# Transposing both heads of a query block before either copy out of PSUM, in a one-core streaming encoder layer

## The chip, the cores and the metric

One core of one Trainium2 chip runs the whole program. The metric is device time in microseconds, median of several runs; the kernel before was run three times.

## The reference

One trunk layer of a streaming encoder for 1024 prompt frames and 64 sample frames, 1024 features, all in fp32:

```python
h = rms_norm(x, norm_mix)
glu_a, glu_b, q, k, v, gates = jnp.split(h @ w_in, SPLITS, axis=-1)
u = glu_a * jax.nn.sigmoid(glu_b)
c, conv_state = causal_dwconv(u, conv_hist, conv_dw, conv_dw_b)          # width 31
c = jax.nn.silu(layer_norm(c, conv_ln_g, conv_ln_b)) @ w_conv_out
a, k_state, v_state = attend(q, k, v, rel_table)                          # 16 heads of 64
a = a @ w_att_out
x = x + (g[..., :D_MODEL] * c + g[..., D_MODEL:] * a) @ w_out
x = x + (jax.nn.gelu(dwconv(up)) * gate) @ w_ffn_down
x = x + jax.nn.sigmoid(rms_norm(x) @ w_ple_gate) * (p @ w_ple_proj)
```

`attend` lets each frame see its own chunk of 64 frames and the eight chunks before it: scores plus a bias by clipped distance, a softmax, and the weighted sum of values. A final norm follows.

## The kernel before

The data lie feature-major: a tile holds 128 features by all 1088 frames. Every big product is done in three passes on TensorE, with weights and activations each split into a high and a low part (`mm3`, lines 154 to 166: high times high, high times low, low times high, over 8 blocks of 128 features). Frames are taken in groups of 384, 384 and 320 columns. ScalarE makes the high parts of the weights (line 134), VectorE the low parts (135).

The first stage, up to about 1 ms, computes the input projection, job by job: a GLU gate and value pair (`gb`, `ga`), gates (`s`), and q, k and v for one pair of heads. It runs two other things beside the projection. One is the depthwise convolution: 31 taps of about 1.4 us on VectorE for each feature block (line 329), later its layer norm on VectorE and ScalarE, kept in a list `bg` that is worked off a little at a time. The other is attention for the pair of heads that is ready: 8 blocks of 128 queries and one of 64 sample queries, held in `pipe`. For each of 8 pairs the 9 query blocks run during the `gb`, `ga` and `s` jobs.

The order is written out by hand: `tick` (line 544) is called twice in each column group of a job, once after the first four feature blocks (12 matmuls) and once after the group's eviction. Ticks alternate. At an even one a new query block's scores are issued (`step_S`), then the weighted sum of an older block (`step_PV`), then the exponentials of the new one (`step_E`). At an odd one an older block is transposed (`step_T`), then the newer one's exponentials are scaled by the reciprocal of their sums (`step_R`). So in steady state TensorE does: transposes of block p, half a projection group, scores of block p+2, weighted sum of block p, the rest of the group, and again.

PSUM has eight banks. Two are for the projection, one for the weighted sum, one for small things. The remaining four are one buffer, `ps_st`, tag "st", with one slot. Scores (`s_ps`, line 478) and transposes (`t_ps`, line 506) use it in turn: head 0 has the first two of its banks, head 1 the other two. A new tile in that slot can be written only once all that used the old one is done. The tile layer that records the instructions adds all waits by itself; it looks at a PSUM tile as a whole here. Each engine runs its own instructions in the order of the program.

The steps by name and line: L485 scores (TensorE, `s_ps`), L491 the bias add and row minimum out of PSUM (VectorE, `s`), L501 exponentials (ScalarE), L526 scaling (ScalarE), L511 transposes (TensorE, `t_ps`; a full block has five of 128 x 128 for each head), L514 the copy of a head's transposes to SBUF (ScalarE, `pt`; L516 and L519 for the sample block), L536 the weighted sum (TensorE, `o_ps`), L170 and L171 its split into high and low parts (`aT`). L677, L662 and L666 are evictions of the `s`, `gb` and `ga` jobs. L159, L160, L161 are the three passes of the projection (`pj`).

Of the kernel before, what the change touches and what calls it, by code (L numbers as in the profile page):

```python
# [75 lines left out]
def encoder_step(ctx: ExitStack, tc: tile.TileContext, I, O):  # L76
# [143 lines left out]
    with tc.manual_schedule():  # L220
# [283 lines left out]
        def step_T(st):  # L504
            m, n = st["m"], st["n"]
            ps = ps_st[0].tile([P, 2, 1024], F32, tag="st", name="t_ps")
            st["pt"] = []
            for h, s in enumerate(st["s"]):
                for b in range(st["nb"]):
                    w = min(P, n - b * P)  # L510
                    nc.tensor.transpose(ps[0:w, h, b * P:b * P + m], s[0:m, b * P:b * P + w], ident[0:m, 0:m])  # L511
                pt = at.tile([P, 640], F32, tag="pt", name="pt", bufs=2)
                if m == P:
                    nc.scalar.activation(out=pt[:, 0:n], in_=ps[:, h, 0:n], func=AF.Copy)  # L514
                else:
                    nc.scalar.activation(out=pt[:, 0:512].rearrange("p (b q) -> p b q", q=P)[:, :, 0:m],  # L516
                                         in_=ps[:, h, 0:512].rearrange("p (b q) -> p b q", q=P)[:, :, 0:m],
                                         func=AF.Copy)
                    nc.scalar.activation(out=pt[0:64, 512:512 + m], in_=ps[0:64, h, 512:512 + m], func=AF.Copy)  # L519
                st["pt"].append(pt)  # L520
# [23 lines left out]
        def tick(base=1.95):  # L544
# [24 lines left out]
            if flip is not None:  # L569
                step_T(flip)  # L570
                stages["pv"].append(flip)
# [1078 lines left out]
```

## Time and profile before

| what | value |
|---|---|
| runs of the kernel before | 2201.48, 2203.5, 2205.72 us; median 2203.5 |
| the profiled execution | 2199.4 us, its span 2197.3 us |
| granted TensorE clock over the span | 0.99 |
| TensorE, matmuls | 2094.6 us busy, 95% |
| TensorE, weight loads | 2012.2 us busy, 92% |
| VectorE | 1320.1 us busy, 60% |
| ScalarE | 829.8 us busy, 38% |
| GpSimd | 224.2 us busy, 10% |
| attention's transposes | first at 98.8 us, last at 996.8 us |

PE is a matmul on TensorE, PEld a weight load on it; the two overlap. DVE is VectorE, ACT ScalarE, POOL GpSimd, SP SyncE. A group of instructions is given by line, engine, operation, and output and input tiles; "idle before" is the time its engine stood still just ahead of it, and the arrow names what ended that wait. Matmul ends are modelled, so short gaps on PE are less certain than starts.

### The profile page before, as it was taken

What the parts mean: (1) busy time and instruction counts of PE and PEld (TensorE: products, weight loads), DVE (VectorE), ACT (ScalarE), POOL (GpSimd) and SP (SyncE); (2) the same over time, 40 slices, a digit from 0 to 9 for tenths busy, and PEclk for the clock granted to TensorE, in tenths of its full rate; (3) what the DMA queues carried; (4) which work ended last, traced back from release to release, by engine and by line L of the source; (5) the groups of instructions that cost most, each with busy time, mean ns of one, the idle gap of its engine ahead of it and who ended that gap; (6) DMA issues with size and microseconds to landing.
All of it is one profiled execution on the core that took longest, in us unless ns stands there. A gap on an engine that the chain in (4) does not pass through costs nothing.

```text
span 2197.3 us, 35659 instructions
## 1 busy us (share of the span) xinstructions
PE 2094.6 (95%) x14696; PEld 2012.2 (92%) x14696; DVE 1320.1 (60%) x2246; ACT 829.8 (38%) x1583; POOL 224.2 (10%) x453
## 2 busy tenths in 40 slices
PE   8989899999999998979999999999999999999997
PEld 6979798988888887869999999999999999999997
DVE  6676676676766645343235457777777763345644
ACT  5352635344545446473012334333333331113421
POOL 4000101101010111111000000000000020000400
PEclk9999999999999999999999999999999999999999
DMA  3312121212121221113533341212212144331011
GB/s 135 106 35 90 64 86 49 94 50 87 51 90 47 92 76 67 58 54 134 200 128 133 118 138 40 89 69 80 89 60 89 71 161 165 123 121 45 11 58 53
DMA packets 64706, 192.54 MB, mean 88 GB/s; under 512 B 8368, under 2 KB 22976, under 8 KB 63200
## 3 DMA queue, kind: packets, MB, share of 16 engines
q1 hardware_dynamic: 43072, 104.00, 13.8%
q0 software_dynamic: 21328, 85.71, 10.9%
q8 instruction: 115, 1.88, 0.4%
q10 hardware_dynamic: 144, 0.56, 0.1%
q14 instruction: 47, 0.39, 0.1%
HBM read 146.18 MB, written 54.01 MB: 91 GB/s over the span
## 4 chain that ended last, share of the span: by engine, by line
PE 82%; ACT 7%; DVE 5%; issue 4%; DMA 1%; POOL 0%; SPq 0%; POOLq 0%; ACTq 0%; DVEq 0%
PE pj L159 15%; PE pj L161 14%; PE pj L160 14%; PE pj L1159 7%; PE pj L1160 7%; PE pj L1158 7%; PE pj L1461 3%; PE pj L1460 3%; PE pj L1459 3%; PE o_ps L536 2%; PE t_ps L511 2%; PE s_ps L485 2%; ACT pt L514 2%; ACT s L501 1%; DVE c L329 1%
## 5 line engine op out<-in xcount | busy, mean ns | idle before, releaser
L159 PE MATMUL pj<-hT,whl 128*128 128x384 f32 (+1 forms) x1296 | 444.3, 343 | 0.7 <-ACT sg L677 0.7
L160 PE MATMUL pj<-hT,whl 128*128 128x384 f32 (+1 forms) x1296 | 427.0, 329 | 0.0
L161 PE MATMUL pj<-hT,whl 128*128 128x384 f32 (+1 forms) x1296 | 426.7, 329 | 0.3 <-DVE whl L135 0.3
L329 DVE SCALAR_TENSOR_TENSOR c<-u,cc,c 128x1118 f32<-128x1118 f32 x240 | 330.7, 1378 | 2.4
L159 PEld LDWEIGHTS pj<-hT,whl 128*128 128x128 f32 x1296 | 246.2, 190 | 14.2 <-issue 10.9
L161 PEld LDWEIGHTS pj<-hT,whl 128*128 128x128 f32 x1296 | 245.8, 190 | 0.6 <-DVE whl L135 0.6
L160 PEld LDWEIGHTS pj<-hT,whl 128*128 128x128 f32 x1296 | 245.9, 190 | 0.0
L1158 PE MATMUL pj<-mp,wq 128*128 128x272 f32 x704 | 204.2, 290 | 5.0 <-ACT ug L1234 2.7
L1160 PE MATMUL pj<-mp,wq 128*128 128x272 f32 x704 | 204.6, 291 | 0.0
L1159 PE MATMUL pj<-mp,wq 128*128 128x272 f32 x704 | 204.4, 290 | 0.0
L135 DVE TENSOR_TENSOR whl<-raw,whl 128x1024 fp32r<-128x1024 f32 (+3 forms) x100 | 115.8, 1159 | 137.0 <-ACT whl L134 136.9
L134 ACT ACTIVATE whl<-raw 128x1024 fp32r<-128x1024 f32 (+3 forms) x100 | 100.1, 1001 | 221.5 <-PE pj L1461 133.7
L491 DVE CUSTOM_DVE_ANT_0 s<-s_ps,bias 128x640 f32<-128x640 f32 (+3 forms) x144 | 90.4, 664 | 145.2 <-PE s_ps L485 145.0
L1135 ACT ACTIVATE wq<-raw 128x512 fp32r<-128x512 f32 x144 | 84.3, 625 | 191.0 <-DVE raw L1144 135.6
L511 PE MATMUL t_ps<-ident,s 128*128 128x128 f32 (+2 forms) x560 | 86.7, 277 | 71.9 <-ACT pt L514 66.8
L511 PEld LDWEIGHTS t_ps<-ident,s 128*128 128x128 f32 (+2 forms) x560 | 61.9, 141 | 92.0 <-ACT pt L514 82.5
L1460 PE MATMUL pj<-gp,whl 128*128 128x384 f32 (+1 forms) x432 | 141.3, 327 | 0.3 <-DVE gp L1369 0.3
L1461 PE MATMUL pj<-gp,whl 128*128 128x384 f32 (+1 forms) x432 | 141.3, 327 | 0.2 <-DVE whl L135 0.2
L1459 PE MATMUL pj<-gp,whl 128*128 128x384 f32 (+1 forms) x432 | 141.0, 326 | 0.0
L1158 PEld LDWEIGHTS pj<-mp,wq 128*128 128x128 f32 x704 | 134.1, 191 | 5.4 <-ACT ug L1234 2.9
L1159 PE MATMUL pj<-bq,wq 128*128 128x272 f32 x480 | 138.6, 289 | 0.0
L1160 PE MATMUL pj<-bq,wq 128*128 128x272 f32 x480 | 138.3, 288 | 0.0
(255 smaller groups left out, 4716.9 us busy)
## 6 DMA issues: line engine op xcount, KB each, us to landing
raw<-in_w_in SPq DMA_DIRECT2D x56, 512.0 KB, 3.5
raw<-in_w_ffn_up SPq DMA_DIRECT2D x44, 512.0 KB, 4.5
q_d<-ug POOLq DMA_DIRECT2D x22, 544.0 KB, 3.0
gp<-q_d POOLq DMA_DIRECT2D x22, 544.0 KB, 7.3
tg<-s_d POOLq DMA_DIRECT2D x16, 544.0 KB, 3.9
aP<-a_d POOLq DMA_DIRECT2D x8, 1088.0 KB, 6.0
a_d<-aT POOLq DMA_DIRECT2D x64, 128.0 KB, 2.2
f_d<-e_d POOLq DMA_DIRECT2D x16, 383.5 KB, 4.9
```

The source lines that it names most:

```text
L135: nc.vector.tensor_tensor(out=hl[:, 1, 0:k, :], in0=raw[:, 0:k, :], in1=hl[:, 0, 0:k, :].bitcast(F32), op=ALU.subtract)
L159: nc.tensor.matmul(ps, lhsT=wsel(hl, 0, k), rhs=r[:, 0, c0:c0 + n], start=(k == 0), stop=False)
L160: nc.tensor.matmul(ps, lhsT=wsel(hl, 0, k), rhs=r[:, 1, c0:c0 + n], start=False, stop=False)
L161: nc.tensor.matmul(ps, lhsT=wsel(hl, 1, k), rhs=r[:, 0, c0:c0 + n], start=False, stop=(k == K - 1))
L329: nc.vector.scalar_tensor_tensor(out=c_t[f], in0=u_t[f][:, j:j + CCOL], scalar=pc("conv_dw", f * CW + j), in1=c_t[f], op0=ALU.mult, op1=AL ...
L511: nc.tensor.transpose(ps[0:w, h, b * P:b * P + m], s[0:m, b * P:b * P + w], ident[0:m, 0:m])
L1158: nc.tensor.matmul(ps, lhsT=q[:, 0, kt, :], rhs=h, start=start and kt == 0, stop=False)
L1159: nc.tensor.matmul(ps, lhsT=q[:, 0, kt, :], rhs=l, start=False, stop=False)
L1160: nc.tensor.matmul(ps, lhsT=q[:, 1, kt, :], rhs=h, start=False, stop=stop and kt == 3)
L1459: nc.tensor.matmul(ps, lhsT=hl[:, 0, k, :], rhs=h, start=k == 0, stop=False)
L1460: nc.tensor.matmul(ps, lhsT=hl[:, 0, k, :], rhs=l, start=False, stop=False)
L1461: nc.tensor.matmul(ps, lhsT=hl[:, 1, k, :], rhs=h, start=False, stop=k == K - 1)
```

## The change

In `step_T` the loop over the two heads is cut in two. The transposes of both heads are issued first, in the same order as before, and then the two copies, in the same order as before.

```diff
             for h, s in enumerate(st["s"]):
                 for b in range(st["nb"]):
                     w = min(P, n - b * P)
                     nc.tensor.transpose(ps[0:w, h, b * P:b * P + m], s[0:m, b * P:b * P + w], ident[0:m, 0:m])
+            for h in range(2):
                 pt = at.tile([P, 640], F32, tag="pt", name="pt", bufs=2)
                 if m == P:
                     nc.scalar.activation(out=pt[:, 0:n], in_=ps[:, h, 0:n], func=AF.Copy)
```

Without the waits, every engine's list of instructions is the same in both programs. What differs is what some of them wait for. On TensorE, around the transposes of one full query block and the next scores, the program before has (in brackets the semaphores of the engines that are waited for):

```order
L511 MATMUL t_ps<-ident,s 128x128 [waits DVE_49,PE_49,Activation_49]
L511 MATMUL t_ps<-ident,s 128x128 x4
L511 MATMUL t_ps<-ident,s 128x128 [waits Activation_49]
L511 MATMUL t_ps<-ident,s 128x128 x4
L159 MATMUL pj<-hT,whl 128x384
...
L161 MATMUL pj<-hT,whl 128x384
L485 MATMUL s_ps<-K,Q 128x320 [waits Activation_49]
L485 MATMUL s_ps<-K,Q 128x320 x11
```

and the changed one, at the same place:

```order
L511 MATMUL t_ps<-ident,s 128x128 [waits DVE_49,PE_49,Activation_49]
L511 MATMUL t_ps<-ident,s 128x128 x4
L511 MATMUL t_ps<-ident,s 128x128 [waits Activation_49]
L511 MATMUL t_ps<-ident,s 128x128 x4
L159 MATMUL pj<-hT,whl 128x384
...
L161 MATMUL pj<-hT,whl 128x384
L485 MATMUL s_ps<-K,Q 128x320 [waits PE_49,Activation_49]
L485 MATMUL s_ps<-K,Q 128x320 x11
```

Nothing moved. The second head's first transpose names ScalarE's semaphore in both, but the count differs: before, it is the count that head 0's copy L514 reaches; now, the one that the scaling L526 of head 1's scores reaches. The scores L485 also name TensorE's own semaphore now, at the count of the last transpose.

On ScalarE, around the copies of one full query block, before (each of the two copies waits for TensorE):

```order
L501 ACTIVATE s,sm<-s,sm 128x640 [waits DVE_49] x2
L677 ACTIVATE sg<-pj,cc 128x320 [waits DMASW4_49,PE_49]
L514 ACTIVATE pt<-t_ps 128x640 [waits PE_49,Activation_49] x2
L526 ACTIVATE s<-s,sm 128x640 [waits DVE_49] x2
L170 ACTIVATE aT<-o_ps 128x128 [waits DMASW7_49,PE_49]
```

and now, with line numbers one higher from the added line on:

```order
L501 ACTIVATE s,sm<-s,sm 128x640 [waits DVE_49] x2
L678 ACTIVATE sg<-pj,cc 128x320 [waits DMASW4_49,PE_49]
L515 ACTIVATE pt<-t_ps 128x640 [waits PE_49,Activation_49]
L515 ACTIVATE pt<-t_ps 128x640 [waits Activation_49]
L527 ACTIVATE s<-s,sm 128x640 [waits DVE_49] x2
L170 ACTIVATE aT<-o_ps 128x128 [waits DMASW7_49,PE_49]
```

The first copy's wait for TensorE is now at the count of the last transpose of head 1, and the second copy waits for TensorE no more.

## The prediction

> **What bounds the kernel now.** I read the page's busy line first, then busy time by stage, then TensorE's waits, then one quiet query block and one disturbed one in the timeline. The page:
>
> ```profile
> PE 2094.6 (95%) x14696; PEld 2012.2 (92%) x14696; DVE 1320.1 (60%) x2246; ACT 829.8 (38%) x1583; POOL 224.2 (10%) x453
> ...
> L511 PE MATMUL t_ps<-ident,s 128*128 128x128 f32 (+2 forms) x560 | 86.7, 277 | 71.9 <-ACT pt L514 66.8
> ```
>
> TensorE is the bound, with 2094.6 of 2197.3 us busy, and about 102.7 us idle. One line, the transposes, has 71.9 of that. By stage (start and end; length; busy time and count of PE, PEld, DVE, ACT, POOL; granted clock; DMA share; GB/s):
>
> ```profile
> 99.00:917.00 818.00, 760.76 (x5502) 699.75 (x5501) 522.47 (x828) 384.33 (x835) 87.67 (x172) 1.00 0.21 69
> 917.00:997.00 80.00, 64.18 (x461) 56.61 (x459) 35.48 (x72) 57.12 (x101) 9.87 (x16) 0.91 0.15 52
> 997.00:2197.00 1200.00, 1179.52 (x8229) 1175.34 (x8228) 696.44 (x1240) 347.22 (x561) 95.70 (x219) 0.99 0.28 99
> ...
> 223.00:287.00 64.00, 56.93 (x452) 49.55 (x450) 43.02 (x78) 39.27 (x85) 8.52 (x15) 1.00 0.17 57
> 287.00:343.00 56.00, 55.92 (x359) 54.49 (x359) 38.23 (x48) 15.57 (x38) 4.48 (x11) 1.00 0.26 90
> ```
>
> The change can act only before 997 us. There, stretches with attention in them (223 to 287) leave TensorE idle for 7 of 64 us; the projections between them (287 to 343) leave 0.1 us. After 997 it is 98% busy. Who it waits for, in the quiet attention stretches (to 917) and in the last one (917 to 997), where ScalarE also carries the layer norm's passes:
>
> ```profile
> PE t_ps L511 <- ACT pt L514: 51.6, 56, 4.4
> PE t_ps L511 <- ACT pt L519: 4.4, 7, 0.6
> PE v_ps L708 <- ACT lnb L384: 1.2, 2, 0.6
> ...
> PE t_ps L511 <- ACT pt L514: 15.2, 8, 2.6
> PE t_ps L511 <- ACT pt L519: 0.6, 1, 0.6
> ```
>
> Total, times, longest. That is 63 waits and 56.0 us to 917, 9 waits and 15.8 us after it: 72, one for each of the 8 x 9 query blocks. Each stands between head 0's transposes and head 1's. A quiet block of full size (start, duration, engine, line, idle before and its releaser):
>
> ```profile
> 501.27 0.64 PEld L511 LDWEIGHTS t_ps<-ident,s 128*128 128x128 f32 x5
> 501.44 0.71 PE L511 MATMUL t_ps<-ident,s 128*128 128x128 f32 x5
> 501.64 0.58 ACT L677 ACTIVATE sg<-pj,cc 128x384 f32<-128x384 f32 x1 [0.38 <-PE pj L161]
> 502.25 0.70 ACT L514 ACTIVATE pt<-t_ps 128x640 f32<-128x640 f32 x1
> 503.00 0.53 PEld L511 LDWEIGHTS t_ps<-ident,s 128*128 128x128 f32 x5 [1.09 <-ACT pt L514]
> 503.00 0.77 PE L511 MATMUL t_ps<-ident,s 128*128 128x128 f32 x5 [0.85 <-ACT pt L514]
> 503.50 0.19 PEld L159 LDWEIGHTS pj<-hT,whl 128*128 128x128 f32 x1
> 503.87 0.70 ACT L514 ACTIVATE pt<-t_ps 128x640 f32<-128x640 f32 x1 [0.92 <-PE t_ps L511]
> 504.47 1.54 ACT L526 ACTIVATE s<-s,sm 128x640 f32<-128x640 f32 x2
> 505.80 0.89 PEld L485 LDWEIGHTS s_ps<-K,Q 64*128 64x128 f32 x12 [0.25 <-issue]
> 508.13 0.82 DVE L491 CUSTOM_DVE_ANT_0 s<-s_ps,bias 128x640 f32<-128x640 f32 x1
> 508.99 0.83 ACT L501 ACTIVATE s<-s,sm 128x640 f32<-128x640 f32 x1 [0.47 <-DVE sm L491]
> 510.34 0.71 PE L511 MATMUL t_ps<-ident,s 128*128 128x128 f32 x5
> ```
>
> Five transposes, a pause of TensorE of 0.85 us while ScalarE copies head 0, five more; then ScalarE in turn idles 0.92 us before copying head 1. The two engines take turns on one four-bank tile, though each head has two banks of its own in it. A block comes every 510.34 - 501.44 = 8.90 us. (Line numbers are those of the kernel before.)
>
> **The pause.** Issue order is the same on all five engines; only waits change. Head 1's first transpose now waits for the scaling L526 of its own scores, made one period earlier, so nothing in front of it is late. Removed per block: by the PE row 0.85 us, by the weight-load row 1.09. The pipe also drains and refills, so I take 0.05 above the PE row. To 917: 56.0 + 63 x 0.05 = 59.2 us. Ends: 56, and 71 if every load gap counted in full, from
>
> ```profile
> PEld t_ps L511 <- ACT pt L514: 65.4, 56, 4.6
> ...
> PEld t_ps L511 <- ACT pt L519: 5.6, 7, 0.8
> ```
>
> **The copies move together.** Head 0's copy now waits for all the transposes. Five loads of 0.14 us take 0.64, so one each 0.125 us; five more delay it by 0.63: it starts at 502.25 + 0.63 = 502.88, the second ends 1.40 later at 504.28, and TensorE sees it some 0.05 us after (502.95 to 503.00 above). Who waits? The next scores, L485, which reuse the same four banks. Their place comes forward too: ten loads from 501.27 end at 502.52, and from the first projection load to theirs it was 503.50 to 505.80, so they want to start at 504.82. Slack about 0.5 us, where it was 505.80 - 504.57 = 1.2. In the groups of 320 columns the half group of twelve matmuls is about a sixth shorter, 0.35 us by proportion, and the slack 0.15. The cover is those twelve projection matmuls; without them each block would pay 1.4 us. Queued behind the copies on ScalarE are the scaling L526, a weight split L134 and the copy aT L170; they come earlier by up to 0.3 us, since ScalarE loses its 0.92 us between copies. GpSimd's and SyncE's queues are not passed by anything.
>
> What does not fit under that cover? The blocks where ScalarE is late already. The longest, at 136.7:
>
> ```profile
> 136.33 4.21 DVE L329 SCALAR_TENSOR_TENSOR c<-u,cc,c 128x1118 f32<-128x1118 f32 x3
> 136.49 0.64 PEld L511 LDWEIGHTS t_ps<-ident,s 128*128 128x128 f32 x5
> 140.63 0.49 ACT L662 ACTIVATE u<-pj 128x384 f32<-128x384 f32 x1 [4.15 <-DVE c L329]
> 141.02 0.70 ACT L514 ACTIVATE pt<-t_ps 128x640 f32<-128x640 f32 x1
> 141.77 1.33 PE L511 MATMUL t_ps<-ident,s 128*128 128x128 f32 x5 [4.40 <-ACT pt L514]
> 145.82 0.89 PEld L485 LDWEIGHTS s_ps<-K,Q 64*128 64x128 f32 x12 [0.25 <-issue]
> ```
>
> Three taps on VectorE hold ScalarE's eviction L662, and the copies stand behind it. After the change they would still run from 141.02 to 142.42, while the scores want 136.49 + 1.25 + 2.30 = 140.04: 2.4 us of the 4.40 come back as a wait of L485. For the other late blocks and the 320-column groups I allow 3 us (some 21 blocks of 63 at 0.1, and a few tenths for the rest; 0 to 10). To 917: 59.2 - 2.4 - 3 = 54 us.
>
> **The new wait.** L485 now also waits on TensorE's own semaphore, an instruction of its own ahead of it in 48 places; the transposes carry such a one already:
>
> ```profile
> L511 PEldq EVENT_SEMAPHORE  x71: 51/51/51, 98.8 to 992.6; - x71
> ```
>
> 51 ns, and at 501.27 no gap in the loads before it. What it waits for is twelve matmuls old. I take nothing; 48 x 0.051 = 2.4 us is the other end.
>
> **The last stretch, 917 to 997.** Here the pauses average 15.8 / 9 = 1.76 us, and the granted clock is 0.91. The rows of one pause:
>
> ```profile
> 926.06 0.64 PE L511 MATMUL t_ps<-ident,s 128*128 128x128 f32 x2 [1.88 <-ACT pt L514]
> 926.81 0.52 PE L160 MATMUL pj<-hT,whl 128*128 128x384 f32 x1
> 927.13 0.52 PE L161 MATMUL pj<-hT,whl 128*128 128x384 f32 x1
> ...
> 929.82 0.33 PE L161 MATMUL pj<-hT,whl 128*128 128x384 f32 x1
> ```
>
> After 1.88 us of idle time matmuls take 0.52 us instead of 0.33 for a while, so a pause costs more than itself; over the stretch up to 0.09 x 80 = 7.2 us. The Trainium skill, "TensorE: Matmul & The Clock Gate", section "HAM oscillation — how this bites in real kernels", has the clock fall only when a gap crosses a window of about 3.4 us. By that rule only the 4.40 us pause would cost clock, the stretch would give back only part of its 15.8 us of pauses, an estimated 10, and the sum would be 64. The row at 926.06 shows a fall after a shorter pause, and the measurement decides. But ScalarE is busy 57.12 of 80 us, so the stretch can't go below 57: gain at most 22.9. At least it should give 9 x 0.9 = 8. I take 14, the stretch at 66 us with ScalarE 87% busy, a little below the middle since each score group must pass VectorE, exponentials, layer-norm passes and copies in series.
>
> **The sum.** 54 + 14 = 68 us. The profiled execution took 2199.4 us (span 2197.3): 2131 for it. The median of the runs shown is 2203.5, 4.1 above the profiled one; against it, 2135.5, my number. After 997 us nothing changes: TensorE is full, and order and buffers are the same.
>
> **Rivals.**
> *The pause moves to the scores.* The slack of 0.15 to 0.5 us is small; if copies end 0.4 us late beyond it at a typical block, 63 x 0.4 = 25 us come back: 43 gained, 2160. For: both copies now sit in one block ahead of L485. Against: in the quiet rows ScalarE is free before the transposes end (0.58 us of eviction ends at 502.22). The Trainium skill, "Perfetto Trace Analysis", section "Optimizing Scalar/DVE Operations", speaks for this rival: where ScalarE isn't saturated but makes bubbles elsewhere, instructions broken up finer let work end sooner, and here two copies that alternated with transposes become one lump; no run shows it yet. Chance 0.12.
> *VectorE and ScalarE become the pace.* In 223 to 287 VectorE is busy 43.02 of 64, which would be 43 of 57, 75%; the bias add L491 queues behind convolution taps (1.4 us each, 4.21 for the three above), and the exponentials behind it (508.13 and 508.99 on in the quiet rows, where they end just before the next block's first copy is due at 510.34 + 0.81). If half of the 54 is lost and the last stretch gives 8: 35 gained, 2168. Chance 0.10.
> *Nothing happens.* Engine order is identical, so if the wait between the heads survived in another form, the time is 2203.5. Against: the built program's count for that wait is that of the scaling. Chance 0.02.
> *Slower.* L485 waits for more than the pause cost. Saved per block 0.9, slack 0.5: ScalarE would have to bring the copies 1.4 us later than reckoned at the average of 72 blocks. At 2 us it is 72 x 0.6 = 43 us more, 2247. The average lateness even in the last stretch is 1.76 - 0.85 = 0.9 us, and a late ScalarE delays the old order as well. Chance 0.03.
> *More.* No cover fails, a block gives 1.0 us (between the 0.85 and the 1.09), and ScalarE fills the last stretch: 63 + 22.9 = 86 gained, 2117. Chance 0.05.
>
> **The numbers.** My forecast has the remaining 0.68. The range runs from 2117 (the last rival) to 2160 (the first); outside lie the second rival and the two behind it, 0.15, and little below. A change within 0.2% (4.4 us), which this measurement can hardly tell from none, needs the pause to survive: 0.02. Slower 0.03, faster 0.95.
>
> **What would show it.** Right: the row of L511 on TensorE loses its 71.9 us to ScalarE (a few us left); ten transposes in a run of some 1.3 us; two copies back to back with no wait between them; a stretch like 223 to 287 of 57 us; clock near 1.00 in the last stretch; new waits of L485 on ScalarE of about 5 us in all to 917. Wrong: L485 waiting 20 us or more for L515 (first rival), E's start L501 late behind VectorE (second), L511 still waiting for the copy (third), or gains and losses after the attention.

## The result, and the profile after

The changed kernel takes 2117.57 us, median of 4 runs (2116.73 to 2118.39). The kernel before took 2204.61, median of 4 runs (2201.48 to 2207.33), the three shown above among them. The ratio is 0.9606, with a 95% interval of 0.9589 to 0.9622: 87 us faster. The time lies at the lower edge of the predicted range, 18 us below the predicted number and next to the rival "More".

The page's busy line after:

```profile
PE 2075.9 (98%) x14696; PEld 2005.9 (95%) x14696; DVE 1318.6 (62%) x2246; ACT 822.6 (39%) x1583; POOL 225.2 (11%) x453
```

The line of the transposes, with its 71.9 us of idle time, is gone from the page's costliest groups. By stage, before (start and end; length; busy time and count of PE, PEld, DVE, ACT, POOL; granted clock; DMA share; GB/s), cut ahead of the first transposes of all, ahead of the last pair's first ones, and behind its last:

```profile
98.99:917.82 818.83, 761.59 (x5507) 700.56 (x5505) 523.30 (x830) 385.16 (x838) 87.67 (x172) 1.00 0.21 69
917.82:996.96 79.14, 63.32 (x456) 55.78 (x453) 34.66 (x70) 56.30 (x99) 9.87 (x16) 0.91 0.15 52
996.96:2197.30 1200.34, 1179.56 (x8230) 1175.36 (x8228) 696.44 (x1240) 347.22 (x561) 95.70 (x219) 0.99 0.28 99
```

and after, cut at the same places of the program; the last row is the attention stretch that was 223 to 287:

```profile
98.77:854.54 755.77, 748.90 (x5507) 699.45 (x5505) 522.34 (x830) 379.43 (x838) 87.67 (x172) 1.00 0.22 75
854.54:914.22 59.68, 56.24 (x456) 49.90 (x453) 34.66 (x70) 54.38 (x97) 9.87 (x16) 1.00 0.19 66
914.22:2114.90 1200.68, 1180.58 (x8230) 1176.37 (x8228) 696.35 (x1240) 347.74 (x563) 95.69 (x219) 0.99 0.28 100
...
209.00:266.00 57.00, 57.00 (x463) 51.34 (x462) 43.83 (x82) 39.73 (x86) 8.39 (x15) 1.00 0.19 65
```

The first stage lost 818.83 - 755.77 = 63.06 us, the last pair's stretch 79.14 - 59.68 = 19.46, the rest of the program nothing (1200.34 against 1200.68). That is 82.5 us; the span fell by 82.4. What went is of two kinds. Idle time of TensorE fell from 57.2 to 6.9 us in the first stage and from 15.8 to 3.4 in the last. But its busy time fell too, by 12.7 and 7.1 us, though it runs the same 5507 and 456 matmuls. The stretch of 57 us has no idle time left.

The block that the prediction showed at 501.44, after the change (start, duration, engine, line, idle before):

```profile
467.91 1.19 PEld L511 LDWEIGHTS t_ps<-ident,s 128*128 128x128 f32 x10
468.08 1.25 PE L511 MATMUL t_ps<-ident,s 128*128 128x128 f32 x10
468.28 0.58 ACT L678 ACTIVATE sg<-pj,cc 128x384 f32<-128x384 f32 x1 [0.38 <-PE pj L161]
...
469.43 1.30 ACT L515 ACTIVATE pt<-t_ps 128x640 f32<-128x640 f32 x2 [0.57 <-PE t_ps L511]
470.65 1.55 ACT L527 ACTIVATE s<-s,sm 128x640 f32<-128x640 f32 x2
471.38 0.89 PEld L485 LDWEIGHTS s_ps<-K,Q 64*128 64x128 f32 x12 [0.25 <-issue]
```

Ten transposes run in 1.25 us without a break, and the two copies follow one another. From the first transpose's load to the next scores' load it was 505.80 - 501.27 = 4.53 us and is now 471.38 - 467.91 = 3.47: 1.06 less. The copies end at 469.43 + 1.30 = 470.73, and the scores, which need their banks, start loading at 471.38 for another reason ("issue"): the copies are covered with 0.65 us to spare.

What TensorE still waits for around the shared banks (total, times, longest), to 854 and from there to 914.5:

```profile
PE s_ps L485 <- ACT pt L515: 3.5, 3, 2.4
PE t_ps L511 <- DVE sm L491: 2.2, 7, 0.5
...
PE s_ps L485 <- ACT pt L515: 2.0, 3, 0.8
PE t_ps L511 <- DVE sm L491: 1.3, 2, 0.8
```

Of 72 pauses of 71.8 us, 15 waits of 9.0 us are left. The longest is the late block of the prediction, where three taps on VectorE hold an eviction on ScalarE:

```profile
131.67 4.21 DVE L329 SCALAR_TENSOR_TENSOR c<-u,cc,c 128x1118 f32<-128x1118 f32 x3
...
132.01 1.25 PE L511 MATMUL t_ps<-ident,s 128*128 128x128 f32 x10
...
135.98 0.49 ACT L663 ACTIVATE u<-pj 128x384 f32<-128x384 f32 x1 [4.16 <-DVE c L329]
136.37 1.30 ACT L515 ACTIVATE pt<-t_ps 128x640 f32<-128x640 f32 x2
137.72 1.14 PE L485 MATMUL s_ps<-K,Q 64*128 64x320 f32 x12 [2.36 <-ACT pt L515]
```

Of its 4.40 us, 2.36 are back as a wait of the scores; the prediction had 2.4.

### The profile page after: what moved, and what is told of

It is laid out like the page before. It is cut to its first block, busy times and chain, and to the rows that moved or that the text cites. A ratio compares the mean times of both kernels' runs of the same rounds, so it can differ in the third digit from the quotient of the medians.

```text
span 2114.9 us, 35643 instructions
## 1 busy us (share of the span) xinstructions
PE 2075.9 (98%) x14696; PEld 2005.9 (95%) x14696; DVE 1318.6 (62%) x2246; ACT 822.6 (39%) x1583; POOL 225.2 (11%) x453
## 4 chain that ended last, share of the span: by engine, by line
PE 87%; DVE 5%; ACT 4%; issue 3%; DMA 0%; POOL 0%; SPq 0%; POOLq 0%; DVEq 0%; ACTq 0%
PE pj L159 16%; PE pj L161 15%; PE pj L160 15%; PE pj L1160 7%; PE pj L1161 7%; PE pj L1159 7%; PE pj L1461 3%; PE pj L1462 3%; PE pj L1460 3%; PE o_ps L537 3%; PE s_ps L485 2%; PE t_ps L511 2%; DVE c L329 1%; DVE acc L1006 1%; DVE s L491 1%
## 5 line engine op out<-in xcount | busy, mean ns | idle before, releaser
L491 DVE CUSTOM_DVE_ANT_0 s<-s_ps,bias 128x640 f32<-128x640 f32 (+3 forms) x144 | 90.3, 663 | 90.2 <-PE s_ps L485 90.0
L1460 PE MATMUL pj<-gp,whl 128*128 128x384 f32 (+1 forms) x432 | 140.9, 326 | 0.0
L1159 PEld LDWEIGHTS pj<-mp,wq 128*128 128x128 f32 x704 | 133.8, 190 | 5.4 <-ACT ug L1235 2.9
L1160 PE MATMUL pj<-bq,wq 128*128 128x272 f32 x480 | 138.5, 289 | 0.0
L1161 PE MATMUL pj<-bq,wq 128*128 128x272 f32 x480 | 138.3, 288 | 0.0
L1159 PE MATMUL pj<-bq,wq 128*128 128x272 f32 x480 | 138.2, 288 | 0.0
L1160 PEld LDWEIGHTS pj<-mp,wq 128*128 128x128 f32 x704 | 133.7, 190 | 0.0
```

The costliest lines, as they stand in the source:

```text
L491: nc.vector.tensor_tensor_reduce(out=s[0:m, 0:n].rearrange("p (x c) -> p x c", x=nh), in0=ps[0:m, h, 0:nh, 0:w], in1=c["bias"][h][0:m, b0: ...
L1159: nc.tensor.matmul(ps, lhsT=q[:, 0, kt, :], rhs=h, start=start and kt == 0, stop=False)
L1160: nc.tensor.matmul(ps, lhsT=q[:, 0, kt, :], rhs=l, start=False, stop=False)
L1161: nc.tensor.matmul(ps, lhsT=q[:, 1, kt, :], rhs=h, start=False, stop=stop and kt == 3)
L1460: nc.tensor.matmul(ps, lhsT=hl[:, 0, k, :], rhs=h, start=k == 0, stop=False)
```

## The experiments

The theory: TensorE paused because the tile layer tracks the four banks as one tile, so head 1's transposes waited for head 0's copy; the new order takes the pause away and hides both copies under the projection matmuls ahead of the next scores. The rivals differ by experiment and stand in what was expected. Where a kernel does more or less than the reference needs, it is said; all others compute the same.

**Banks of their own, old order.** The kernel before, with one tile of two banks for each head, for scores and transposes, and the old order of the lines:

```diff
-            ps = ps_st[0].tile([P, 2, 2, 512], F32, tag="st", name="s_ps")
+            ps = [ps_st[0].tile([P, 2, 512], F32, tag=f"st{h}", name="s_ps") for h in range(2)]
...
-            ps = ps_st[0].tile([P, 2, 1024], F32, tag="st", name="t_ps")
+            ps = [ps_st[0].tile([P, 1024], F32, tag=f"st{h}", name="t_ps") for h in range(2)]
...
```

> The old order of the lines, but the four-bank tile is two tiles of two banks, one for each head, for scores and for transposes. Theory (the pause is a wait on the whole tile, since head 1's transposes go to other banks than the copy reads): the pause goes without any reordering, and the scores and transposes wait only for their own head's banks, which can save some of the 9 us of waits that the changed kernel has left on L485 and L511: 2108 to 2118 us. Rival (the order of issue, copies after all the transposes, is what brings the gain): it stays within 10 us of 2204.6.

Measured: 2114.65 us (2113.77 to 2116.71) beside 2201.62 for the kernel before; ratio 0.9603 (0.9589 to 0.9618). The old order gains as much as the new one. Its waits on TensorE for these banks:

```profile
PE s_ps L485 <- ACT pt L514: 4.9, 8, 1.8
```

No transpose waits for a copy, though each copy still stands in the code between the two heads. So it was the common tile, not the place of the lines. Order matters only because it decides at which count of the other engine the common tile's wait is set.

**The last pair alone.** The new order for pair 7, the old one for pairs 0 to 6:

```diff
...
+            ahead = st["i"] == 7
+            if ahead:
+                turn_head(0)
+                turn_head(1)
+            for h in range(2):
+                if not ahead:
+                    turn_head(h)
```

> Both heads' transposes ahead of the copies for the last pair of heads only; pairs 0 to 6 keep the old order. Theory (TensorE's pause between the heads is what the time was, and long pauses also cost clock): only the last attention stretch shrinks, by the 19.5 us by which it shrank in the changed kernel, 79.2 to 59.8; so 2204.6 - 19.5 = 2185 us, give or take 3. Rival (what counts is that ScalarE's copies come in a run and free it for everything behind them, about the same for each block): 9 of 72 blocks' share of 82 us, 10 us, so 2194 us.

Measured: 2182.89 us (2180.86 to 2184.44) beside 2201.62; ratio 0.9909 (0.9892 to 0.9925), 18.7 us less. That agrees with the 19.5 us of the trace for this stretch. Pairs 0 to 6 wait as before:

```profile
PE t_ps L512 <- ACT pt L522: 51.8, 56, 4.4
```

**How much of that is the clock.** The kernel before, with nine matmuls between the two heads of pair 7 (blocks 1 to 7), so that TensorE works through the pause. It computes more than the reference needs; their result is thrown away:

```diff
+                if h == 0 and st["i"] == 7 and 0 < st["p"] < 8:
+                    fp = ps_m.tile([P, 512], F32, tag="m", name="fill")
+                    for _ in range(9):
+                        nc.tensor.matmul(fp[:, 0:384], lhsT=hT[0][:, 0, 0:P], rhs=hT[0][:, 0, 0:384], start=True,
+                                         stop=True)
```

> The kernel before, with nine projection-like matmuls (about 1.55 us) into an unused bank in the pause between the heads, for the last pair's seven prompt blocks after the first; their result is thrown away. The pauses there are 1.9 to 2.6 us long, so the filler should fit. Theory (these pauses lower the granted clock for a while, which made up about 6 of the last stretch's 19.5 us): the pause remains, but matmuls behind it keep 0.34 us, the stretch's clock goes from 0.91 to about 1.00, and the time falls by 4 to 7 us, to about 2196 where the kernel before has 2201.6. Rival (the rule that the clock falls only after some 3.4 us without work, so that the slow matmuls have another cause, or the filler only delays the transposes): no change or up to 3 us more.

Measured: 2196.09 us (2193.76 to 2200.32) beside 2205.0; ratio 0.9968 (0.9959 to 0.9978), about 7 us less by the ratio for 63 added matmuls. The last stretch and one filled pause:

```profile
923.04:996.05 73.01, 68.07 (x519) 60.09 (x516) 34.59 (x70) 56.38 (x99) 9.90 (x16) 1.00 0.17 56
```

```profile
956.22 1.83 PE L515 MATMUL fill<-hT 128*128 128x384 f32 x9
958.34 0.77 PE L511 MATMUL t_ps<-ident,s 128*128 128x128 f32 x5 [0.28 <-ACT pt L519]
```

The granted clock of the stretch is 1.00 where it was 0.91, and the stretch 79.14 - 73.01 = 6.1 us shorter, though the pauses are still there, only filled. So some 6 to 7 of the 19.5 us are clock, most of the rest is idle time. As a whole the two profiled executions differ by only 1.0 us (spans of 2196.3 and 2197.3): in the one with the filler, matmuls behind three unfilled pauses of earlier pairs (at 495.8, 810.0 and 856.9) took 0.52 us, and in the other they did not. Which pauses lower the clock thus differs from run to run, and the 7 us rest on the 11 and 15 runs, not on these two traces. The pauses in this stretch average 1.76 us, and the longest took 2.6. The Trainium skill, "TensorE: Matmul & The Clock Gate", section "HAM oscillation — how this bites in real kernels", has the clock fall when TensorE idles across a window of about 3.4 us; by that rule filling pauses shorter than the window would have changed nothing here, and the 7 us speak against it. Counting the transposes on both sides of a pause as no work either does not save the rule: from the first transpose to the next projection matmul, the kernel before has 2.55, 3.29, 3.10 and 4.23 us in this stretch where matmuls behind took 0.52 us, and 2.94, 3.15 and 3.22 us where they did not. Only one of the seven is over 3.4 us, so length alone does not decide; what does stays open.

**Head 0's copy twice, old order.** The kernel before, with one more copy in each prompt block; the second writes the same again:

```diff
-                    nc.scalar.activation(out=pt[:, 0:n], in_=ps[:, h, 0:n], func=AF.Copy)
+                    for _ in range(2 - h):
+                        nc.scalar.activation(out=pt[:, 0:n], in_=ps[:, h, 0:n], func=AF.Copy)
```

> The kernel before, with head 0's copy done twice in the prompt's blocks. Theory: TensorE stands still for all of the added copy, 0.65 us at a full block (two copies in a run take 1.30), less at the four smaller ones: about 4.1 us a pair, 33 us in all, and somewhat more for clock lost after longer pauses: 2235 to 2250 us. Rival (ScalarE has time to spare and the copy is hidden): under 10 us more.

Measured: 2245.75 us (2242.46 to 2249.76) beside 2201.62; ratio 1.0198 (1.0181 to 1.0216), 44 us more. The transposes' wait:

```profile
PE t_ps L511 <- ACT pt L515: 105.6, 64, 5.1
```

The page of before has 66.8 there: 38.8 more for 64 copies, 0.61 us each. In the old order nothing hides a copy of head 0. The other 5 us go with the clock, 0.988 over the span where it was 0.990, and were not traced further.

**The same in the new order.** The edit above on the changed kernel.

> The changed kernel, with head 0's copy done twice in the prompt's blocks. Theory (the twelve projection matmuls between transposes and scores cover the copies with 0.15 to 0.5 us to spare): of the added 0.65 us a full block passes on 0.15 where a 384-column group follows and 0.5 where a 320-column one does, 0.27 on average, 9 us over 32 full blocks, some 3 us more in the last stretch: 2126 to 2133 us. Rival (no cover: what ScalarE gets is paid by TensorE): 33 us more, 2151 us. Second rival (slack well above 0.65): no change, 2118 us.

Measured: 2136.18 us (2134.95 to 2138.51) beside 2201.62; ratio 0.9701 (0.9687 to 0.9716). The span is 2133.1 against 2114.9, 18.2 us more, and the time 3 us over the expected range: the cover hides a little more than half of the added copy. The wait is now at the scores; in the matmul's rows, then in the weight loads':

```profile
PE s_ps L485 <- ACT pt L516: 14.7, 18, 3.1
PE t_ps L511 <- DVE sm L491: 6.7, 15, 0.7
...
PEld s_ps L485 <- ACT pt L516: 26.3, 34, 3.4
```

**Both copies twice, new order.**

```diff
-                    nc.scalar.activation(out=pt[:, 0:n], in_=ps[:, h, 0:n], func=AF.Copy)
+                    for _ in range(2):
+                        nc.scalar.activation(out=pt[:, 0:n], in_=ps[:, h, 0:n], func=AF.Copy)
```

> The changed kernel, with both copies of a prompt block done twice: 1.30 us more on ScalarE at a full block, 66 us in all. Theory (a cover of fixed size: of the first 33 us added, 18 came through, and beyond the cover all does): 18 + 33 = 51 us over the changed kernel, 2165 to 2180 us. Rival (ScalarE as a whole becomes the pace of the stage, so the exponentials and scalings behind the copies come late as well): over 66 us more, 2185 us and above.

Measured: 2167.51 us (2164.94 to 2169.61) beside 2205.0; ratio 0.984 (0.9824 to 0.9855); the span is 2167.7, 52.8 us above the changed kernel's. Its waits, matmuls and loads:

```profile
PE s_ps L485 <- ACT pt L516: 38.3, 34, 3.8
...
PEld s_ps L485 <- ACT pt L516: 51.1, 47, 4.1
PEld o_ps L538 <- ACT pt L516: 6.2, 9, 1.1
```

The first added copy costs 18.2 us, the second 34.6: of 64 times 0.61 us, 39 in all, the cover takes 21 from the first and 4 from the second. So it is nearly used up after one more copy. The rows also tell how to price a wait. All of attention, from its first transposes to the matmul behind its last, in the changed kernel, with one copy doubled and with both (columns as above):

```profile
98.77:914.22 815.45, 805.13 (x5961) 749.35 (x5958) 557.00 (x899) 433.81 (x933) 97.54 (x188) 1.00 0.22 74
...
99.99:933.95 833.96, 808.96 (x5961) 750.58 (x5958) 557.58 (x899) 469.51 (x997) 97.52 (x188) 1.00 0.22 73
...
99.45:968.25 868.80, 816.44 (x5961) 756.00 (x5958) 558.22 (x899) 505.17 (x1061) 97.83 (x188) 0.99 0.21 70
```

With one copy doubled this stretch is 18.5 us longer; the idle time between matmuls rose by 14.7 us (10.3 to 25.0), that between weight loads by 17.3 (66.1 to 83.4). With both doubled it is 53.4 us longer, with 42.0 more between matmuls and 46.7 more between loads. In both, the loads' gaps are nearer to the cost, and neither is all of it.

**No cover.** The changed kernel with the transposes moved to the tick of the next scores, directly ahead of them, so that no projection matmul stands between. It computes the same, in another order:

```diff
-                if stages["pv"]:
-                    done = stages["pv"].pop(0)
-                    spent += 0.218 * done["nb"] + 0.2
-            elif stages["t"]:
-                flip = stages["t"].pop(0)
-                spent += 0.214 * flip["nb"]
+                if len(stages["t"]) >= 2 or (stages["t"] and new is None):
+                    flip = done = stages["t"].pop(0)
+                    spent += 0.432 * done["nb"] + 0.2
+                    step_T(flip)
...
-            if flip is not None:
-                step_T(flip)
-                stages["pv"].append(flip)
```

> The changed kernel, with each block's transposes moved directly ahead of the next scores: at an even tick come the transposes of an older block, the new block's scores, the weighted sum of the older block; no projection matmuls stand between transposes and scores any more. (The convolution's pace in the list is reckoned from the same work, but at other ticks.) Theory (what the change gains is that twelve projection matmuls run while ScalarE copies): TensorE now waits at the scores for both copies, 1.30 us and some 0.15 of latency at a full block, less at the small ones, about 10.8 us a pair, 86 us in all: the whole gain is given back, 2195 to 2215 us. Rival (the gain comes from the ten transposes in a run and the copies in a run): it stays within 15 us of 2117.6.

Measured: 2257.36 us (2255.33 to 2258.56) beside 2205.0; ratio 1.0248 (1.023 to 1.0266). The direction is as expected, the size isn't: not 86 us come back but 140, and the kernel is slower than before. Its waits on TensorE, and all of attention:

```profile
PE s_ps L485 <- ACT pt L515: 99.1, 56, 5.1
PE o_ps L537 <- ACT pt L515: 12.9, 16, 2.5
```

```profile
100.06:1056.39 956.33, 838.59 (x5961) 780.89 (x5959) 559.16 (x899) 434.68 (x933) 98.39 (x189) 0.97 0.19 63
```

Two blocks, the first with a longer wait, the second a clean one:

```profile
526.48 1.55 ACT L527 ACTIVATE s<-s,sm 128x640 f32<-128x640 f32 x2 [1.14 <-DVE sm L571]
...
527.93 1.28 ACT L515 ACTIVATE pt<-t_ps 128x640 f32<-128x640 f32 x2
...
529.26 1.97 PE L485 MATMUL s_ps<-K,Q 64*128 64x320 f32 x12 [2.89 <-ACT pt L515]
...
540.03 1.14 PE L485 MATMUL s_ps<-K,Q 64*128 64x320 f32 x12 [1.39 <-ACT pt L515]
```

The clean block waits 1.39 us, which is the 1.4 of the prediction for a block without cover. The other waits 2.89, since its copies now stand behind the newer block's scaling on ScalarE, and its scores then take 1.97 us instead of 1.14: the clock is 0.97 over the stage. Of the 140.9 us by which attention is longer than in the changed kernel, 107.4 are idle time of TensorE (117.7 against 10.3) and 33.5 are longer busy time of the same 5961 matmuls. So this kernel changes three things, the cover, the copies' place on ScalarE and the clock. That the cover is needed is shown by the clean block, which pays 1.39 us where the change saves 1.06; what the cover is worth over the whole kernel isn't settled by this run.

**The best of both, beside the changed kernel.** The changed kernel again, and the one with banks of their own again, beside each other on one chip.

> The changed kernel once more, on the same chip and in the same call as the one with a head's own banks. Theory: 0.960 to 0.961 of the kernel before, as in the first comparison.

Measured: 2116.48 us (2115.15 to 2118.62) beside 2202.24; ratio 0.9605 (0.9591 to 0.9619).

> A head's own banks, old order of the lines, once more. Theory (all the gain is the pause, and both ways remove the same pause): equal to the changed kernel within 0.2%; its transposes no longer wait 3.4 us in all for the bias add of the other head, so 0 to 4 us less. Rival (each head's copy may now start 0.6 us earlier, which relieves the scores in late blocks): 5 us less or more.

Measured: 2114.12 us (2112.93 to 2115.16); ratio 0.9593 (0.9579 to 0.9606). It is 2.4 us below the changed kernel, 0.1%, and the intervals of the ratios overlap. All of its attention:

```profile
99.11:912.25 813.14, 806.70 (x5961) 752.23 (x5958) 557.26 (x899) 431.70 (x934) 97.78 (x188) 1.00 0.23 74
```

TensorE idles 6.4 us there, against 6.9 + 3.4 = 10.3 in the changed kernel: the waits for the bias add L491 are gone, since head 0's transposes need only head 0's scores out of their banks. The stretch is 2.3 us shorter than the 815.45 of the changed kernel, less than the idle time saved, since the busy time is 1.6 us longer. It is the fastest kernel here by the median, and its runs hardly meet those of the changed kernel (2112.93 to 2115.16 against 2115.15 to 2118.62), but with so few runs a gain this small is likely, not certain.

## Why the prediction was right, and where its sizes were off

**What bounds it.** Right. TensorE was the pace, the pause between the heads was the loss, and only the time before 997 us changed.

**The pause was worth more than its row.** This is the step that failed most: "The pipe also drains and refills, so I take 0.05 above the PE row." The idle time was forecast well: 56.0 in pauses less 2.4 + 3 that come back is 50.6 us, and 57.2 - 6.9 = 50.3 went. But busy time fell by 12.7 us in the first stage, 12.7 / 63 = 0.20 us a block where 0.05 was taken for drain and refill. The rows show where most of it sits: two runs of five transposes took 0.71 + 0.77 = 1.48 us, one run of ten takes 1.25, 0.23 less. About 1 us of the 12.7 is clock by the rows behind the 4.40 us pause, where five transposes took 1.33 us and the granted clock was 0.91 from 140 to 160 us. The first stage gave 63.1 us where 54 were forecast. The loads' rows, which the prediction quoted as the other end, were nearer: 65.4 + 5.6 = 71.0, less the 5.4 that come back, is 65.6, and all idle time between loads fell by 62.0 us (118.3 to 56.3). The two kernels with doubled copies say the same of a wait.

**The copies under cover.** Right. In the quiet block they end 0.65 us before the scores load, where 0.5 was reckoned; without cover a clean block waits 1.39, where 1.4 was reckoned. On the average of all blocks there was less to spare: of the copy doubled in the new order 18.2 us came through where some 12 were expected.

**What comes back.** The sum was right and part of its reason wrong. Forecast 2.4 + 3 us to 917; measured 2.36 in the late block, 1.1 in the other waits of L485, and 2.2 in a wait that the prediction didn't have: the first transpose for the bias add L491, which must have read both heads' scores out of the common tile. The kernel before has the same wait for VectorE in its list; there, it seems, the pauses left VectorE the time. That it comes from the common tile is shown by the kernel with banks of their own, which has none of it.

**The new wait on TensorE's own semaphore.** Taken at nothing, and it is nothing. Before, the gap for issue at the loads of L485 was

```profile
PEld s_ps L485 <- issue: 12.5, 53, 0.3
```

and after

```profile
PEld s_ps L485 <- issue: 12.5, 54, 0.3
```

**The last stretch.** Forecast 14 us with ends of 8 and 22.9; measured 19.5. Idle time fell by 12.4 of its 15.8 us and busy time by 7.1, of which 9 x 0.2 = 1.8 would be refill and the rest, 5.3, clock; the kernel with filled pauses gained 6.1 there. ScalarE is busy 54.4 of 59.7 us, 91%, where 87% was put down. What was feared, that each block must pass four steps in series on ScalarE and VectorE, cost 3.3 us of waits in all.

**The sum.** 63.06 + 19.46 = 82.5 us in the traces, against 68. Of the 19.0 us by which the gain of 87.0 exceeds the forecast, the first stage has 9.1, the last 5.5. The other 4.4 show in no stage of these traces: the profiled execution of before lay 5.2 us under the median of the four runs, that of after 0.8 under its own. They go with the clock: in the experiments' runs of the kernel before it is 0.990 or 0.991 in those under 2201 us and 0.986 to 0.988 in those over 2204. Whether the pauses cause that too was not traced.

**The rivals.** "The pause moves to the scores" fell: L485 waits 5.5 us in all for the copies, 8.3 in the loads' rows, not 25. The advice that the prediction set beside it, the Trainium skill's "Perfetto Trace Analysis", section "Optimizing Scalar/DVE Operations", is that breaking instructions up may let work end sooner where ScalarE isn't saturated. It is not tested here, since both kernels issue the same two copies. What changed is that independent matmuls of TensorE run while both copies are made; the kernel with banks of their own gains as much with its copies still alternating. "VectorE and ScalarE become the pace" fell in the first stage, where a stretch of 57 us has no idle TensorE; in the last ScalarE comes near it. "Nothing happens" and "slower" fell. "More" came nearest: worked out, it is 2203.5 - 85.9 = 2117.6, and 2117.57 was measured. That this is so close is partly luck. Its 63 us for the first stage were 63.1, though it let nothing come back and 5.7 us did; its 22.9 for the last stretch were 19.5, and the 3.4 us too much stand against the 4.4 that show in no stage. Its chance of 0.05 was too small: its price per block lay in the middle of two rows that were both on the table, and the forecast's lay at the lower one. The forecast of 68 us was 19 us short, and its range held the result only at its very end.

What stays open: how the 12.7 us of busy time split between filling the pipe, the clock and the way that matmul ends are modelled. That they are real time shows in the length of the stage, not in the busy column alone.

## What to carry to other kernels

When two halves of a buffer are produced and consumed in turn, look whether the layer that sets the waits sees them as one tile: issue all producers ahead of the consumers, or give each half a tile of its own, which here gained the same 4%. Issuing the producers ahead paid here because independent work of the bound engine stood behind them; the version without it, which also moved the copies on ScalarE, ran 2.5% slower than the kernel before. Price a pause of TensorE by the gap in its weight loads rather than by the one in its matmuls (it was nearer in all three comparisons here), and read the granted clock of the stretch for what comes on top.

## What the runs showed of the hardware that was not expected

- Five transposes of 128 x 128 in fp32 cost 0.71 to 0.77 us as a run, ten cost 1.25: in these rows a run interrupted once costs 0.23 us more than its idle time.
- Pauses of 1.76 us on average, 2.6 at most, in one stretch went with a granted clock of 0.91; seven of them filled with nine useless matmuls each brought it to 1.00 and the kernel 7 us down (ratio 0.9968, 0.9959 to 0.9978).
- In the kernel without cover a wait of 2.89 us was followed by scores at 1.97 us instead of 1.14.
